# The first v of an attention-times-value kernel: two halves with two semaphores, cast by two engines

## The chip, the cores and the metric

The kernel runs on one core of one Trainium2 chip. The metric is the device time of one execution in microseconds (us). Three runs of the kernel before gave 1054.49 to 1054.95 us, median 1054.9.

## The reference

```
attn_weights: [8, 12, 1024, 1024] float32
v:            [8, 12, 1024, 64]   float32
out = einsum('bhqs,bhsd->bhqd', attn_weights, v)   # float32
```

For each of the 96 heads a 1024x1024 matrix is multiplied by a 1024x64 matrix. The attention weights are 403 MB, v and the output 25 MB each.

## The kernel before, in words

**Tiling.** Four heads make a group (`NV` = 24 groups). A group's attention weights are handled in two units (`NU` = 48), each with half of the queries of the four heads. A partition holds 32 queries of one head, so that 128 partitions hold four heads; a unit has `G` = 16 query slots of each partition. One load of a unit (`load_attn`, L314 to L320) reads 8 MB of float32 and writes 4 MB of bf16 into one of two buffers `abf`: the transfer itself converts. It is issued by GpSimd (POOL), whose transfers run on the software queue, q0. The last two units are loaded in two halves.

**A unit.** PE waits for its buffer, then transposes the 16 slots in 16 groups of 4 matmuls (`transpose_g`, L130), which use the four PSUM banks 0 to 3 in turn. From group 4 on, PE waits for the copy that empties the bank (`s_cp`). DVE copies the groups 0, 2, 4, 5, 7 of each eight, ACT the others (`copy_g`, L254). In the first unit of a group PE also spreads v (`spread_v`, L145): v arrives as `vr`, in bf16, with 32 rows of each head spread over partitions, and is brought into the layout `vbf` by PE, DVE and ACT (L230). Then the previous unit's result is transposed back (L157) and copied to `osb` (L237), and the unit's products are made (L172) and copied to `ot` (L266).

**What sets the order.** Each engine has its own instruction queue. POOL issues loads 0 and 1 at once, builds the constants `ident` and `spread` with affine selects, and then runs a loop over n (L363 to L372): it waits until PE has done those of unit n's transposes that DVE copies (`s_t[True]`), and issues load n + 2 into the buffer that these have freed. In some steps it also issues a load of v for two groups (`load_v`, L322) or a store of results.

**The first v.** The v of the first two groups (eight heads) takes another way. SP (SyncE) loads it as float32 on the hardware queue, q1, into two free slots of `osb` (`v32`, from slot `V_SLOT` = 4): first the 128 rows of group 0 (`two` = 0), then group 1 (`two` = 1) as 96, 22 and 10 rows (L382 to L385). A row is 2048 elements, 8 KB. All four transfers count on one semaphore, `s_v0`. DVE clears `ident`, `spread` and `ot`, waits for all four (L305), casts both groups into `vr` at once (L306) and adds 2 to `s_vr`; only after that does it enter its loop over the units. PE waits for `s_vr` of at least 1 before it spreads group 0 (L195), and of at least 2 before it spreads group 1, in unit 2. After its four transfers SP adds to `s_free` and `s_half`, which ACT's copies to `osb` and PE's groups from 8 on wait for.

Of the kernel before, what the change touches and what calls it, by code (L numbers as in the profile page):

```python
# [10 lines left out]
def kernel(  # L11
# [18 lines left out]
    nc = tc.nc  # L30
# [7 lines left out]
    P = 128  # L38
# [15 lines left out]

    NO = 8 + 2
    V_SLOT = 4

    HALVED = NU - 2

    def slot(q):  # L60
        return q % NO
# [6 lines left out]
    v_2 = v.rearrange("b h q d -> (b h) q d").rearrange(  # L68
        "(hq two four) (p r) d -> hq (four p) two (r d)", two=2, four=VH, p=VP
    )  # L70

    def on_dve(g):
        return g % 8 in (0, 2, 4, 5, 7)

    def count_of(g):

        return sum(on_dve(x) == on_dve(g) for x in range(g + 1))
# [4 lines left out]
    with tc.tile_critical(sync_engine=mybir.EngineType.Pool, no_gpsimd_drain=True):  # L82
        sem = tc.alloc_semaphore
# [5 lines left out]
        vr = sb("vr", [P, 2, VB, SB * D], bf16)  # L89
        vbf = sb("vbf", [P, SB, VH, D], bf16)  # L90
        ot = sb("ot", [P, GH, P], fp32)
        osb = sb("osb", [P, NO, 2 * G, D], fp32)

        v32 = osb[:, ds(V_SLOT, 2)].rearrange("p n r d -> p (n r d)")
        bank = [nc.alloc_psum_tensor(f"bank{i}", [P, 512], fp32).ap() for i in range(8)]
        pt = [b.rearrange("p (k j) -> p k j", k=KW) for b in bank[:4]]
        po = bank[4:6]
# [2 lines left out]

        s_abf = [sem(f"s_abf{i}") for i in range(2)]
        s_second = {n: sem(f"s_second{n}") for n in range(HALVED, NU)}
        s_v0, s_v = sem("s_v0"), sem("s_v")
        s_osb = [sem(f"s_osb{i}") for i in range(2)]
        s_held, s_end = sem("s_held"), sem("s_end")

# [11 lines left out]
        s_memset, s_const, s_vr = sem("s_memset"), sem("s_const"), sem("s_vr")  # L118
# [100 lines left out]
        transpose_back()  # L219


        def engine(dve):
            eng = nc.vector if dve else nc.scalar
            copy = nc.vector.tensor_copy if dve else nc.scalar.copy
            per = PER_DVE if dve else PER_ACT
            e = 0 if dve else 1

            def spread_copy(h, ps, count):
                eng.wait_ge(s_sp[e], count)
                copy(  # L230
                    out=vbf[:, :, h], in_=ps.rearrange("p (k d) -> p k d", k=SB)
                ).then_inc(s_vbf[e])

            def back_copy(rows, j0, jn, ps, count):

                eng.wait_ge(s_back, count)
                return copy(  # L237
                    out=rows.rearrange("p (half j) d -> p j half d", half=2)[:, ds(j0, jn)],
                    in_=ps[:, ds(0, jn * P)].rearrange("p (j half d) -> p j half d", half=2, d=D),
                )  # L240

            def rows_of(n):
                return osb[:, slot(n // 2), ds(n % 2 * G, G)]

            def back_copies(rows, count, free=None):
                if free is not None:
                    eng.wait_ge(s_free, free)
                for k in range(2):
                    last = back_copy(rows, 4 * k, 4, px[k], count + k + 1)
                last.then_inc(s_out)  # L250

            def copy_g(g, count):
                eng.wait_ge(s_t[dve], count)  # L253
                ins = copy(  # L254
                    out=at[:, g].rearrange("c k j two -> c (k j two)"),
                    in_=bank[g % 4].bitcast(bf16),
                )
                if g < G - 4:
                    ins.then_inc(s_cp[g])
                elif g == (G - 1 if dve else G - 2):  # L260
                    ins.then_inc(s_last[e])

            def product(count):

                eng.wait_ge(s_m[e], count)
                copy(  # L266
                    out=ot.rearrange("c j (h p) -> c h j p", h=VH)[:, ds(2 * e, 2)],
                    in_=po[e].rearrange("c (h j p) -> c h j p", h=2, j=GH),
                ).then_inc(s_ot[e])

            mine = [g for g in range(G) if on_dve(g) == dve]

            def unit(n, base, rows, free):

                of_t, of_sp, of_back, of_m = base
                for g in mine:
                    copy_g(g, of_t + (n * per + count_of(g)))
                if n % 2 == 0:
                    spread_copy(e, po[e], of_sp + (n + 1))
                    spread_copy(2 + e, px[e], of_sp + (n + 2))  # L280
                if not dve:
                    back_copies(rows, of_back + 2 * n, free)
                product(of_m + (n + 1))


            with nc.Fori(1, NV + 1, 1, engines=(DVE if dve else ACT,)) as it:  # L286
                base = [eng.snap(it * (2 * k) - 2 * k) for k in (per, 1, 2, 1)]
                rows = [None, None]
                if not dve:
                    for n, q in enumerate((it + (NO - 2), it + (NO - 1))):  # L290
                        rows[n] = osb[:, ds(eng.snap(q % NO), 1), ds((1 - n) * G, G)].rearrange(
                            "p one r d -> p (one r) d"
                        )
                    free = eng.snap((it + 1) // 2)
                unit(0, base, rows[0], None)
                unit(1, base, rows[1], None if dve else free)
            k = 1 - e
            back_copy(rows_of(NU - 1), 4 * k, 4, px[k], 2 * NU + k + 1).then_inc(s_fin[k])
# [3 lines left out]

        for h in range(2):
            nc.vector.memset(ot[:, :, ds(h * HP, HP)], 0.0).then_inc(s_ot[h])
        nc.vector.wait_ge(s_v0, 16 * 4)  # L305
        nc.vector.tensor_copy(out=vr.rearrange("p two b x -> p (two b x)"), in_=v32).then_inc(s_vr, 2)  # L306
        engine(True)
        engine(False)
        nc.scalar.wait_ge(s_held, 16 * (BY_SYNC - HELD_FROM) // 2)


        pool = nc.gpsimd

        def load_attn(n):  # L314
            pieces = [(0, G)] if n < HALVED else [(0, GH), (GH, GH)]
            for g0, gn in pieces:
                pool.dma_start(  # L317
                    out=abf[n % 2][:, ds(g0, gn)].rearrange("p g s -> p (g s)"),
                    in_=attn_q[n // 2][:, ds((n % 2 * G + g0) * S, gn * S)],
                ).then_inc(s_abf[n % 2] if g0 == 0 else s_second[n], 16)  # L320

        def load_v(iv):  # L322
            pool.dma_start(  # L323
                out=vr.rearrange("p two b x -> p two (b x)"), in_=v_2[iv]
            ).then_inc(s_v, 16)
# [10 lines left out]
        def store_2(q):  # L336
            store(q, 2, pool, s_osb[q // 2 % 2] if q < HELD_FROM else s_held)
# [5 lines left out]
            out=ident,  # L343
            in_=ident,
# [7 lines left out]
        for h in range(VH):  # L352
            pool.wait_ge(s_const, h + 1)
            pool.affine_select(  # L354
                out=spread[ds(h * VP, VP)],
                in_=spread[ds(h * VP, VP)],
# [6 lines left out]
        for n in range(NU - 2):  # L363
            q, i = n // 2, n % 2
            if i == 0 and q % 2 == 1 and q + 1 < NV:
                for s in s_sp:
                    pool.wait_ge(s, 2 * q + 2)
                load_v((q + 1) // 2)
            pool.wait_ge(s_t[True], (n + 1) * PER_DVE)
            load_attn(n + 2)  # L370
            if i == 0 and q % 2 == 0 and 0 < q <= HELD_FROM:
                store_2(q - 2)  # L372
        for q in range(HELD_FROM, BY_SYNC, 2):
# [4 lines left out]

        v32_2 = v32.rearrange("p (two x) -> p two x", two=2)
        for two, p0, pn in ((0, 0, P), (1, 0, 96), (1, 96, 22), (1, 118, 10)):  # L382
            nc.sync.dma_start(  # L383
                out=v32_2[ds(p0, pn), two], in_=v_2[0][ds(p0, pn), two]
            ).then_inc(s_v0, 16)  # L385
        nc.sync.sem_inc(s_free, NO // 2)
        nc.sync.sem_inc(s_half, HALVED)
        for k in range(1, NV // 2):
# [12 lines left out]
        for k in range(2):  # L401
# [3 lines left out]
            out=out_q[NV - 1], in_=osb[:, slot(NV - 1)].rearrange("p r d -> p (r d)")  # L405
# [32 lines left out]
```

## Time and profile before

| what | value |
|---|---|
| median of three runs | 1054.9 us (1054.49 to 1054.95) |
| the profiled execution | 1054.56 us |
| its span, first to last instruction | 1052.7 us |
| PE, matmuls busy | 737.3 us, 70% |
| PE, weight loads busy | 691.3 us, 66% |
| DVE busy | 388.5 us, 37% |
| ACT busy | 425.6 us, 40% |
| POOL busy | 45.0 us, 4% |
| HBM read and written | 427.82 MB and 25.17 MB |
| mean granted TensorE clock | 0.868 |

Issuing the 50 attn loads takes POOL 27.2 us. The median time from issue to landing of an attn load of 4096 KB is 33.5 us, of a later v load 17.2 us.

In a timeline line the columns are: start in us, duration in us, engine, line, operation, destination and source, shapes, count, and in brackets the idle time before it with what ended it. PE is the matmul row, PEld its weight loads, which overlap it. In the chain of waits the columns are start, duration, and what was waited for. "DMA" in the chain means the time from the issue of a transfer to its landing, which includes any time that the transfer stood in a queue. In the page's queue lines the numbers are packets, MB and the time that the packets took as a share of 16 DMA engines over the span (or over the window asked for).

### The profile page before, as it was taken

The numbers are of one execution on the slowest core, as the hardware profiler recorded it, in microseconds if no ns is written. First come the engines' busy times: TensorE is split into PE (matmuls) and PEld (weight loads), VectorE is DVE, ScalarE is ACT, GpSimd is POOL, SyncE is SP. The second block draws the span as 40 slices with busy tenths as digits, with TensorE's granted clock in tenths as the row PEclk, the third lists the DMA queues.
The fourth block names the chain that finished last, engine by engine and source line by source line (L and its number), as shares of the span: only waits on it lengthen the run. The fifth ranks groups of instructions, "written<-read, shape, count | busy, mean of one in ns | idle before, by whom it ended". The sixth has DMA issues, their size and how long they took to land.

```text
span 1052.7 us, 16498 instructions
## 1 busy us (share of the span) xinstructions
PE 737.3 (70%) x6920; PEld 691.3 (66%) x6920; DVE 388.5 (37%) x582; ACT 425.6 (40%) x505; POOL 45.0 (4%) x80
## 2 busy tenths in 40 slices
PE   0877677577686568766669657776776875875895
PEld 0776676576686567656668657765666865875884
DVE  0443343333353234333335324433333433532452
ACT  0454354343353334433335434433333443543452
POOL 1000000000000000000000000000000000000000
PEclk9989788898798888889879888888988988988898
DMA  9999999999999999999999999999999999999998
GB/s 237 221 219 214 217 252 217 219 217 247 228 213 254 215 219 257 218 218 225 240 220 217 258 217 219 257 214 217 246 224 219 218 208 229 215 210 222 214 215 344
DMA packets 13784, 240.17 MB, mean 228 GB/s; under 512 B 1237, under 2 KB 1237, under 8 KB 4053
## 3 DMA queue, kind: packets, MB, share of 16 engines
q0 software_dynamic: 12912, 233.84, 99.1%
q1 hardware_dynamic: 869, 6.29, 1.5%
q8 instruction: 2, 0.03, 0.0%
q14 instruction: 1, 0.01, 0.0%
HBM read 427.82 MB, written 25.17 MB: 430 GB/s over the span
## 4 chain that ended last, share of the span: by engine, by line
DMA 76%; PE 22%; issue 1%; DVE 0%; SPq 0%; ACT 0%; POOL 0%; DVEq 0%; POOLq 0%
DMA abf<-in_attn_weights_dram 73%; PE bank L130 21%; DMA osb<-in_v_dram 3%; PE bank L172 1%; PE bank L157 0%; DVE vbf L230 0%; SPq L383 0%; PE bank L145 0%; DVE at L254 0%; DVE osb L237 0%; ACT ot L266 0%; POOL abf L317 0%; DVEq L253 0%; DVE vr L306 0%; DVEq L286 0%
## 5 line engine op out<-in xcount | busy, mean ns | idle before, releaser
L130 PE MATMUL bank<-ident,abf 128*128 128x128 f32 x3072 | 453.5, 318 | 274.0 <-DMA abf<-in_attn_weights_dram 269.4
L130 PEld LDWEIGHTS bank<-ident,abf 128*128 128x128 f32 x3072 | 443.4, 214 | 287.4 <-DMA abf<-in_attn_weights_dram 281.2
L254 DVE COPY at<-bank 128x1024 bf16<-128x1024 bf16 x480 | 320.1, 689 | 466.1 <-PE bank L130 464.3
L254 ACT COPY at<-bank 128x1024 bf16<-128x1024 bf16 x288 | 288.7, 1012 | 404.3 <-PE bank L130 404.2
L172 PE MATMUL bank<-at,vbf 128*64 128x256 bf16 x3072 | 215.0, 278 | 0.0
L172 PEld LDWEIGHTS bank<-at,vbf 128*64 128x64 bf16 x3072 | 196.7, 108 | 13.3 <-DVE at L254 4.0
L266 ACT COPY ot<-bank 128x512 f32<-128x512 f32 x48 | 28.1, 586 | 174.0 <-PE bank L172 174.0
L266 DVE COPY ot<-bank 128x512 f32<-128x512 f32 x48 | 33.2, 692 | 151.3 <-PE bank L172 151.3
L157 PE MATMUL bank<-ident,ot 128*128 128x128 f32 x392 | 52.2, 276 | 32.9 <-DVE vbf L230 32.2
L157 PEld LDWEIGHTS bank<-ident,ot 128*128 128x128 f32 x392 | 43.4, 141 | 45.0 <-DVE vbf L230 44.0
L237 ACT COPY osb<-bank 128x512 f32 (+1 forms) x97 | 52.2, 589 | 27.3 <-PE bank L157 26.1
L317 POOL DMA_DIRECT2D abf<-in_attn_weights_dram x50 | 27.2, 545 | 690.9 <-PE bank L130 689.9
L230 DVE CAST vbf<-bank 128x512 bf16<-128x512 f32 x48 | 30.9, 686 | 6.6 <-PE bank L145 6.6
L254 ACT ACT_TABLE_LOAD x24 | 30.8, 1283 | 1.4 <-PEq L422 1.0
L230 ACT CAST vbf<-bank 128x512 bf16<-128x512 f32 x48 | 25.8, 589 | 11.8 <-PE bank L145 11.8
L145 PE MATMUL bank<-vr,spread 32*128 32x512 bf16 x384 | 25.7, 377 | 0.0
L323 POOL DMA_DIRECT2D vr<-in_v_dram x11 | 7.7, 704 | 238.4 <-PE bank L145 238.4
L145 PEld LDWEIGHTS bank<-vr,spread 32*128 32x128 bf16 x384 | 9.9, 92 | 6.9
L306 DVE CAST vr<-osb 128x4096 bf16<-128x4096 f32 x1 | 2.3, 2294 | 28.3 <-DMA osb<-in_v_dram 28.3
L330 POOL DMA_DIRECT2D out_dram<-osb x10 | 7.1, 715 | 29.8 <-ACT osb L237 29.8
L354 POOL TENSOR_SCALAR_AFFINE_SELECT spread<-spread 32x512 bf16<-32x512 bf16 x4 | 2.5, 628 | 0.6
L237 DVE COPY osb<-bank 128x512 f32<-128x512 f32 x1 | 0.7, 690 | 3.1 <-PE bank L157 3.1
(8 smaller groups left out, 2.1 us busy)
## 6 DMA issues: line engine op xcount, KB each, us to landing
abf<-in_attn_weights_dram POOLq DMA_DIRECT2D x46, 4096.0 KB, 33.5
out_dram<-osb POOLq DMA_DIRECT2D x10, 2048.0 KB, 29.5
vr<-in_v_dram POOLq DMA_DIRECT2D x11, 1024.0 KB, 17.2
abf<-in_attn_weights_dram POOLq DMA_DIRECT2D x4, 2048.0 KB, 24.0
out_dram<-osb SPq DMA_DIRECT2D x1, 2048.0 KB, 13.7
out_dram<-osb SPq DMA_DIRECT2D x2, 1024.0 KB, 11.4
osb<-in_v_dram SPq DMA_DIRECT2D x1, 1024.0 KB
osb<-in_v_dram SPq DMA_DIRECT2D x1, 768.0 KB
```

The source lines that it names most:

```text
L130: last = pe.matmul(out=pt[g % 4][:, k], lhsT=words[:, k], rhs=ident, is_transpose=True, start=(k == 0), stop=(k == KW - 1),)
L145: last = pe.matmul(out=ps, lhsT=spread[rows, b], rhs=vr[rows, two, b], start=(b == 0), stop=(b == VB - 1),)
L157: last = pe.matmul(out=ps[:, ds(j * P, P)], lhsT=ot[:, j0 + j], rhs=ident, is_transpose=True, start=(j == 0), stop=(j == jn - 1),)
L172: last = pe.matmul(out=outs, lhsT=vbf[:, 2 * kw + par, h], rhs=at[:, ds(half * GH, GH), kw, ds(h * VP, VP), par], start=(n == 0), stop=(n ...
L230: copy(out=vbf[:, :, h], in_=ps.rearrange("p (k d) -> p k d", k=SB)).then_inc(s_vbf[e])
L237: return copy(out=rows.rearrange("p (half j) d -> p j half d", half=2)[:, ds(j0, jn)], in_=ps[:, ds(0, jn * P)].rearrange("p (j half d) -> ...
L254: ins = copy(out=at[:, g].rearrange("c k j two -> c (k j two)"), in_=bank[g % 4].bitcast(bf16),)
L266: copy(out=ot.rearrange("c j (h p) -> c h j p", h=VH)[:, ds(2 * e, 2)], in_=po[e].rearrange("c (h j p) -> c h j p", h=2, j=GH),).then_inc( ...
L317: pool.dma_start(out=abf[n % 2][:, ds(g0, gn)].rearrange("p g s -> p (g s)"), in_=attn_q[n // 2][:, ds((n % 2 * G + g0) * S, gn * S)],).th ...
L323: pool.dma_start(out=vr.rearrange("p two b x -> p two (b x)"), in_=v_2[iv]).then_inc(s_v, 16)
L330: eng.dma_start(out=out_2[q // 2] if fours == 2 else out_q[q], in_=at_slot if fours == 2 else at_slot[:, 0], **({"single_packet": True} if ...
L354: pool.affine_select(out=spread[ds(h * VP, VP)], in_=spread[ds(h * VP, VP)], compare_op=mybir.AluOpType.not_equal, fill=1.0, base=0, patte ...
```

## The change

The transfers of the first v get two semaphores, one for each group of four heads. The first group's 128 rows are loaded as 48 and 80 rows, the second's as 96, 22 and 10 rows as before. DVE waits only for the first group's two transfers and casts only that group. The second group is cast by GpSimd: in the first step of its loop, after it has issued the third attn load (n = 0, load 2), it waits for the second group's three transfers and casts. Each cast adds 1 to `s_vr`.

```diff
+    FIRST_V = ((0, 48), (48, 80)), ((0, 96), (96, 22), (118, 10))
...
-        v32 = osb[:, ds(V_SLOT, 2)].rearrange("p n r d -> p (n r d)")
+        v32 = osb[:, ds(V_SLOT, 2)].rearrange("p n r d -> p n (r d)")
...
-        s_v0, s_v = sem("s_v0"), sem("s_v")
+        s_v0, s_v = [sem(f"s_v0_{i}") for i in range(2)], sem("s_v")
...
+        def cast_v(eng, two):
+            eng.tensor_copy(
+                out=vr[:, two].rearrange("p b x -> p (b x)"), in_=v32[:, two]
+            ).then_inc(s_vr)
...
-        nc.vector.wait_ge(s_v0, 16 * 4)
-        nc.vector.tensor_copy(out=vr.rearrange("p two b x -> p (two b x)"), in_=v32).then_inc(s_vr, 2)
+        nc.vector.wait_ge(s_v0[0], 16 * len(FIRST_V[0]))
+        cast_v(nc.vector, 0)
         engine(True)
...
             pool.wait_ge(s_t[True], (n + 1) * PER_DVE)
             load_attn(n + 2)
+            if n == 0:
+                pool.wait_ge(s_v0[1], 16 * len(FIRST_V[1]))
+                cast_v(pool, 1)
             if i == 0 and q % 2 == 0 and 0 < q <= HELD_FROM:
                 store_2(q - 2)
...
-        v32_2 = v32.rearrange("p (two x) -> p two x", two=2)
-        for two, p0, pn in ((0, 0, P), (1, 0, 96), (1, 96, 22), (1, 118, 10)):
-            nc.sync.dma_start(
-                out=v32_2[ds(p0, pn), two], in_=v_2[0][ds(p0, pn), two]
-            ).then_inc(s_v0, 16)
+        for two in range(2):
+            for p0, pn in FIRST_V[two]:
+                rows = ds(p0, pn)
+                nc.sync.dma_start(
+                    out=v32[rows, two], in_=v_2[0][rows, two]
+                ).then_inc(s_v0[two], 16)
```

## The prediction

> **What bounds the kernel now.** I read first the page's slices and queues, to see which resource is never free, then the chain of waits, then the first 68 us of the timeline and the transfers' landing times. From the page:
>
> ```profile
> span 1052.7 us, 16498 instructions
> ...
> DMA  9999999999999999999999999999999999999998
> ...
> q0 software_dynamic: 12912, 233.84, 99.1%
> q1 hardware_dynamic: 869, 6.29, 1.5%
> ...
> DMA abf<-in_attn_weights_dram 73%; PE bank L130 21%; DMA osb<-in_v_dram 3%; PE bank L172 1%; PE bank L157 0%; DVE vbf L230 0%; SPq L383 0%; PE bank L145 0%; DVE at L254 0%; DVE osb L237 0%; ACT ot L266 0%; POOL abf L317 0%; DVEq L253 0%; DVE vr L306 0%; DVEq L286 0%
> ```
>
> The DMA engines are busy in every slice; PE is busy 70% of the span. The last line seems to say otherwise: it gives PE's transposes (L130) 21%. The chain of waits shows where these shares come from, and the place that the change is about:
>
> ```profile
> 2.26 28.47 DMA osb<-in_v_dram
> ...
> 30.82 0.07 DVE vr L306
> ...
> 33.03 0.69 DVE at L254
> 33.73 0.04 issue
> 33.77 7.84 PE bank L130 x48
> ...
> 57.71 29.10 DMA abf<-in_attn_weights_dram
> 86.81 0.04 issue
> 86.85 7.96 PE bank L130 x64
> ```
>
> The chain walks from a landing to the issue of that transfer, and from there to the transposes that freed its buffer. It does not see that the transfer stood in a queue behind another one. So I check it with the landings, which are the starts of the transposes that a transfer released:
>
> ```profile
> 67.53 9.75 PEld L130 LDWEIGHTS bank<-ident,abf 128*128 128x128 f32 x64 [5.11 <-DMA abf<-in_attn_weights_dram]
> 86.85 7.76 PEld L130 LDWEIGHTS bank<-ident,abf 128*128 128x128 f32 x64 [1.81 <-DMA abf<-in_attn_weights_dram]
> 111.07 10.11 PEld L130 LDWEIGHTS bank<-ident,abf 128*128 128x128 f32 x64 [11.26 <-DMA abf<-in_attn_weights_dram]
> 130.40 7.83 PEld L130 LDWEIGHTS bank<-ident,abf 128*128 128x128 f32 x64 [1.46 <-DMA abf<-in_attn_weights_dram]
> ```
>
> The gaps are 19.32, 24.22 and 19.33 us; the long one has a later v load in it (4.9 us). They do not follow the issues, which come at irregular distances (57.71, 79.87, 95.10 us). A load lands 19.3 us after the load in front of it, whenever it was issued: that is a queue that never runs dry. The number that decides this case is therefore whether it runs dry near the third attn load. For the four loads of the first 60 us the trace gives
>
> ```profile
> DMA to landing us min/median/max: 25.6/28.4/46.0
> ```
>
> The longest is the second load: issued at about 2.1 us, it lands at 48.1. The third is issued at 41.91, **6.2 us before that landing**, and lands 25.6 us later, at 67.5, 19.4 after the second: the same spacing as later. The queue did not run dry there, to 0.1 us.
>
> **What DVE's wait costs now.** From the timeline:
>
> ```profile
> 29.24 3.69 PE L130 MATMUL bank<-ident,abf 128*128 128x128 f32 x16 [29.24 <-DMA abf<-in_attn_weights_dram]
> 30.82 2.29 DVE L306 CAST vr<-osb 128x4096 bf16<-128x4096 f32 x1 [28.25 <-DMA osb<-in_v_dram]
> 33.77 7.84 PE L130 MATMUL bank<-ident,abf 128*128 128x128 f32 x48 [0.84 <-DVE at L254]
> 41.91 0.57 POOL L317 DMA_DIRECT2D abf<-in_attn_weights_dram  x1 [35.66 <-PE bank L130]
> ```
>
> DVE waits for all of v until 30.8, casts until 33.1, and only then empties bank 0, which PE needs for group 4: PE stands 0.84 us. It also keeps PE's transposes slow for longer: they take 12.4 us (29.24 to 41.61), while unit 2, which starts after a pause too but has no such stall, needs 9.75 and 0.1.
>
> **The change, part by part.**
>
> *Removed: DVE's wait for the whole v, and half its cast.* The first 128-row half is 8 rows per DMA engine and goes first. The transfers of the first 6 us, the rate in 40 slices and the two queues:
>
> ```profile
> GB/s 0 0 0 0 0 0 0 0 0 0 0 0 164 55 0 109 109 273 164 218 328 437 218 655 164 655 164 546 328 546 328 546 328 546 328 546 328 382 382 437
> ...
> q1 hardware_dynamic: 178, 1.33, 60.9%
> q0 software_dynamic: 2, 0.07, 5.1%
> ```
>
> The first half is 128 rows of 8 KB and 16 completions, 144 packets; 178 had gone by 6.0 us. Adding up the slices of 0.15 us gives 1.05 MB at about 5.2 us. I take a landing of 6 us; the far bound is some 11 us, two attn packets later on a late engine. DVE's cast halves to about 1.2 us (2294 ns for 4096 elements) and is over by 8, bound 12. DVE is idle from 2.6 to 29, so it lies under that. Then DVE copies group 0 when PE has it, at 29.24 + 3.69/4 = 30.2, not 33.0, and bank 0 is free by 30.9, before PE asks at 32.9. PE gains between 0.84 us (the stall alone) and 2.5 (unit 2's 9.9 us, so transposes until 39.1). I take 2.5, since unit 2 is the nearest row. The third load is issued at 39.4 instead of 41.91. **Worth at the end: 0**, because the work in front of it in the queue lasts until 48.1 either way; the slack grows from 6.2 to 8.7 us. The fourth load's issue also comes earlier (unit 1 starts at its landing, 48.1, not at 49.4: 56.5 instead of 57.7) and stands behind the third until 67.5: 0.
>
> *Added on POOL: a wait and a cast of 128x2048, behind the third load's issue.* The wait is for v's second half, which lands at 30.7 now; one more packet in that queue may add one round behind an attn packet, 2.8 us, so 33.5 at most, before the 39.4 at which POOL gets there. The page has no GpSimd cast. Nearest rows: 512 elements of affine select take 628 ns, so 2.5 us; the dearest per element (128 in 0.29 us) gives 4.6; from below, DVE's 1.2. I take 2.5, because the shape is nearer. POOL is done at 42.5 (41 to 45). Behind the cast stands the fourth load, which waits for unit 1's transposes until 56.5: cover 11.5 us at the dear bound. The cast's result is first read in unit 2, after its transposes, at about 77.4: cover 32 us. DVE's half alone satisfies unit 0's wait. So 0.
>
> [...]
>
> *Changed: SP issues five transfers instead of four.* One issue is 0.41 us and 0.05 between: SP comes 0.46 us later to its two semaphore additions, needed by PE at group 8 and by ACT after 40 us: 0. One more completion packet on 16 engines costs between nothing and a row's 0.36 us (9.5% of 16 x 60 us over 256 rows); I take +0.05, as it carries almost no bytes. The bytes of each engine stay the same. The start may gain: in the line of rates above, the mean from 2.25 to 3.15 us is 200 GB/s, then 414, so 0.9 x (1 - 200/414) = 0.47 us of the DMA engines' time is lost while the engines join in. If this ramp goes with the first transfer's rows, 48 of 128 save 0.47 x 80/128 = 0.3; bounds 0 and 0.47. I take 0.3.
>
> [...]
>
> **Sum**, against the profiled execution (1054.56 us, span 1052.7): -0.3 + 0.05 and zeros = 1054.3. That execution is 0.34 below the median of the runs shown, so the forecast of the median is **1054.6**, its own range 1054.4 to 1055.3 (all bounds together).
>
> **Rivals.** About 0.2%, 2.1 us, is what a measurement of this kernel can tell from no change.
>
> *The chain is right, the earlier issue counts in full.* If the queue was emptier at 42 to 48 us than the landings say, for instance because the DMA engine that ends last had nothing left there, PE's 2.5 us reach the end: 1054.9 - 2.5 - 0.25 = **1052.1**. For it: the chain names v's transfer, the cast and PE's stall in a row. Against it: 19.4 us spacing there, 19.3 elsewhere.
>
> *Slower: GpSimd's cast holds back the third load's packets.* At the start POOL issues load 0 at 1.51 us, runs affine selects until 6.24, and the software queue had only 2 packets by 6.0 us: 4.5 us from issue to packets, perhaps because POOL's other work comes between. If packets of the third load are prepared behind the cast, they begin at 40.0 + cast + up to 4.5. With 2.5 that is 47.0, with 4.6 it is 49.1, 1.0 past the 48.1 where the queue runs dry. From a cast of 3.6 us on it costs, from 5.7 us it costs over 2.1; at 7 us, 51.5, 3.4 lost: **1058.1**. Against it: the start's delay may be the packets' preparation itself. [...]
>
> *It does not do what it says:* the first half lands as late as load 0, since both share the engines. Then DVE starts as now and all stays: 1054.9. The 178 packets speak against it. It is inside the forecast's answer.
>
> **How the numbers follow.** No change 0.64 (forecast 0.58, not doing what it says 0.06), earlier issue counts 0.22, cast holds the load 0.14. The range 1051.9 to 1056.5 holds all of the first, some 0.14 of the second and 0.02 of the third. Faster 0.22, same 0.64, slower 0.14.
>
> **What would show it.** DVE's cast near 6 to 8 us, half as long; no PE stall at 33; third load issued at 39 to 41; GpSimd's cast behind it, 2 to 5 us; and still transposes of unit 2 at 67 to 68 us and all later landings on the old grid. I am wrong if unit 2 starts more than 2 us before or after 67.5, or if the grid's spacing changes.

## The result, and the profile after

The changed kernel takes **1056.0 us** (median of 22 runs, 1055.4 to 1057.0) beside 1054.6 us for the kernel before (22 runs, 1053.76 to 1054.95): a ratio of 1.0014, interval 1.0007 to 1.0020. It is slower by some 1.4 us. That is less than the 0.2% named above, but with this many runs the interval leaves no change out. The profiled execution took 1055.76 us, 1.20 above that of the kernel before; 0.8 of that lies in the span from the first to the last instruction (1053.5 against 1052.7) and 0.4 outside it.

First the part that the change aimed at. From the timeline of the changed kernel:

```profile
7.57 1.23 DVE L224 CAST vr<-osb 128x2048 bf16<-128x2048 f32 x1 [5.00 <-DMA osb<-in_v_dram]
29.47 9.99 PE L131 MATMUL bank<-ident,abf 128*128 128x128 f32 x64 [29.47 <-DMA abf<-in_attn_weights_dram]
39.76 0.57 POOL L323 DMA_DIRECT2D abf<-in_attn_weights_dram  x1 [33.53 <-PE bank L131]
40.38 1.89 POOL L224 CAST vr<-osb 128x2048 bf16<-128x2048 f32 x1
```

All of it works. DVE casts the first group long before PE needs it, the stall of 0.84 us is gone (64 transposes in one piece), the third load is issued at 39.76 and not at 41.91, and GpSimd's cast stands behind it with no wait for v. In the chain of waits v's transfer, the cast and the spread are gone:

```profile
DMA abf<-in_attn_weights_dram 77%; PE bank L131 20%; PE bank L173 0%; PE bank L158 0%; POOL abf L323 0%; DVE osb L243 0%; ACT ot L272 0%; POOLq L443 0%; SPq L406 0%; POOLq L432 0%; POOLq L83 0%
```

And still the end is later. The landings say since when (starts of the transposes that a load released):

```profile
49.43 7.83 PEld L131 LDWEIGHTS bank<-ident,abf 128*128 128x128 f32 x64 [2.40 <-DMA abf<-in_attn_weights_dram]
68.61 9.10 PEld L131 LDWEIGHTS bank<-ident,abf 128*128 128x128 f32 x64 [6.14 <-DMA abf<-in_attn_weights_dram]
87.95 9.29 PEld L131 LDWEIGHTS bank<-ident,abf 128*128 128x128 f32 x64 [2.46 <-DMA abf<-in_attn_weights_dram]
112.19 9.45 PEld L131 LDWEIGHTS bank<-ident,abf 128*128 128x128 f32 x64 [9.74 <-DMA abf<-in_attn_weights_dram]
```

The spacing is the old one (19.18, 19.34, 24.24), but the grid stands 1.08 us later at unit 2 (68.61 against 67.53) and 1.10 at unit 3. The second load already lands at 49.4, where it landed at 48.1, and GpSimd's cast, from 40.4 to 42.3, has no load waiting on it. So the time is lost before the second load has landed, and the first 6 us of the transfers show where:

```profile
GB/s 0 0 0 0 0 0 0 0 0 0 0 0 218 382 273 0 218 328 437 382 382 109 55 164 164 55 382 0 109 218 218 382 218 218 382 109 328 164 273 164
...
q1 hardware_dynamic: 132, 0.95, 70.9%
```

Each number is the rate in 0.15 us, with every packet counted where it starts. Up to 3.15 us it is ahead of the kernel before: 0.39 MB have started, as much as the 48 rows. From 3.15 us on the mean is 195 GB/s where it was 414. By 6.0 us 0.95 MB of v had moved, not 1.33. The missing 0.38 MB at 414 GB/s are 0.92 us, near the 1.08 us of the grid. The first load lands only 0.23 us later (29.46 against 29.23): v's rows that are left over move between the packets of both loads (0.95 MB of v had moved by 6.0 us, 2.02 of the 2.10 MB by 30), and the delay stands in full only where both are through. At the last load it is 0.86 us (1032.55 against 1031.69).

### The profile page after: what moved, and what is told of

It is laid out like the page before. It is cut to its first block, busy times and chain, and to the rows that moved or that the text cites. A ratio compares the mean times of both kernels' runs of the same rounds, so it can differ in the third digit from the quotient of the medians.

```text
span 1053.5 us, 16499 instructions
## 1 busy us (share of the span) xinstructions
PE 733.0 (70%) x6920; PEld 687.3 (65%) x6920; DVE 387.6 (37%) x582; ACT 425.6 (40%) x505; POOL 47.0 (4%) x81
## 4 chain that ended last, share of the span: by engine, by line
DMA 77%; PE 21%; issue 1%; POOL 0%; DVE 0%; ACT 0%; POOLq 0%; SPq 0%
DMA abf<-in_attn_weights_dram 77%; PE bank L131 20%; PE bank L173 0%; PE bank L158 0%; POOL abf L323 0%; DVE osb L243 0%; ACT ot L272 0%; POOLq L443 0%; SPq L406 0%; POOLq L432 0%; POOLq L83 0%
```

## The experiments

Three theories stood against each other. *Rows:* a transfer of a part of the rows, all neighbours, moves at a lower rate than one of all 128 while nothing else is queued (195 GB/s against 414 above), and this makes the loss. *Completions:* each further transfer costs its engines some 1.4 us for its completion, which is the whole loss (1056.0 - 1054.6). These two expect the time of the kernel before when the first group goes in one transfer. *Casts:* the two casts, or the earlier third load, delay the queue.

**One transfer again (e1_whole, and once more as e6_again_whole).**

```diff
-    FIRST_V = ((0, 48), (48, 80)), ((0, 96), (96, 22), (118, 10))
+    FIRST_V = ((0, P),), ((0, 96), (96, 22), (118, 10))
```

> The changed kernel with the first group's 128 rows as one transfer again; two semaphores and the two casts stay. [...] Rival 'casts' (the two casts, GpSimd's above all, or the earlier third load delay the queue): stays at 1056.0, unit 2 at 68.6.

> The changed kernel with the first group's 128 rows as one transfer, once more: it stood 0.6 us above the kernel before at the median, with an interval that holds no change. 'Rows' alone: within 0.4 of the kernel before. If the two casts have a price of their own, 0.4 to 1.0 above it.

Measured: 1055.13 us (before 1054.51; ratio 1.0004, 0.9995 to 1.0013) and, in a second set of runs, 1054.95 (before 1054.62; 1.0004, 0.9995 to 1.0013). DVE's cast starts at 6.06 and 6.27 us, unit 2 at 67.22 and 67.61. Both intervals hold no change, so *casts* falls for the greater part of the loss, and the earlier third load (issued at 38.96 in the second of these) brings nothing. But the medians stand 0.6 and 0.3 us above the kernel before, the first outside the 0.4 that *rows* alone leaves room for, and the single runs show where this rest lies. The median span is 1052.8 and 1052.7 us here, beside 1052.6 and 1052.7 for the kernel before: inside the span nothing is lost, to 0.2 us. Outside the span, the time minus the span, the mean is 2.30 and 2.27 us, beside 1.96 and 1.93. All versions with two semaphores and two casts show this, the changed kernel too (2.25 to 2.33 us), and e2_split_only below, which has neither, does not (1.91). So about 0.35 us of the 1.4 come with the two semaphores and casts and not with the rows. Which of them costs it was not tried and stays open.

**The changed kernel beside it (e7_changed).**

> The changed kernel itself on the same chip as its neighbours here: 1.0 to 1.6 above the kernel before, and 0.8 to 1.4 above the one with 128 rows in one transfer. Theory 'casts' (now of the rest only): the distance to the 128-row kernel is under 0.5.

Measured: 1056.17 us, ratio to before 1.0014 (1.0005 to 1.0023), and 1.2 us above e6_again_whole on the same chip (1056.17 - 1054.95). The whole of this is in the span (median 1053.9 against 1052.7).

**The split alone (e2_split_only)**, in the kernel before:

```diff
-        for two, p0, pn in ((0, 0, P), (1, 0, 96), (1, 96, 22), (1, 118, 10)):
+        for two, p0, pn in ((0, 0, 48), (0, 48, 80), (1, 0, 96), (1, 96, 22), (1, 118, 10)):
...
-        nc.vector.wait_ge(s_v0, 16 * 4)
+        nc.vector.wait_ge(s_v0, 16 * 5)
```

> The kernel before with only its first transfer split into 48 and 80 rows; one semaphore, DVE casts all of v as before. 'Rows' and 'completions': 1056.0, unit 2 starts near 68.6. 'Casts': 1054.6, unit 2 at 67.5.

Measured: **1059.09 us**, ratio 1.0041 (1.0028 to 1.0055). Every theory missed that by 3 us and more. The timeline, DVE and POOL, then PE's weight loads:

```profile
37.73 2.29 DVE L306 CAST vr<-osb 128x4096 bf16<-128x4096 f32 x1 [35.16 <-DMA osb<-in_v_dram]
```

```profile
48.86 0.57 POOL L317 DMA_DIRECT2D abf<-in_attn_weights_dram  x1 [42.61 <-PE bank L130]
```

```profile
40.68 7.69 PEld L130 LDWEIGHTS bank<-ident,abf 128*128 128x128 f32 x48 [7.60 <-DVE at L254]
...
71.94 9.29 PEld L130 LDWEIGHTS bank<-ident,abf 128*128 128x128 f32 x64 [2.58 <-DMA abf<-in_attn_weights_dram]
```

All of v lands at 37.7 us, 6.9 us later than before, although only 0.4 MB more were left over at 6.0 us (0.90 MB had moved, not 1.33). By an estimate each row that did not get away before the attn packets came waits behind one of them, some 2.7 us a row (a load's 19.3 us are 8 packets on each engine, 2.4 us each, and the row's own 0.3 us at 437 GB/s for 16 engines). DVE casts late, PE stands 7.6 us, and the third load is issued at 48.86. The second lands at about 49.6 (the mean of the first two, 37.9 us from issue to landing, and the first at 29.79), so there were 0.7 us in hand, and the third lands 22.3 us behind it, not 19.3. The queue did run dry here. The rates from 44 to 56 us, in slices of 0.3 us:

```profile
GB/s 328 437 0 0 546 0 0 437 328 437 0 0 0 0 0 0 0 0 0 0 874 437 328 109 0 0 0 0 0 0 328 1311 109 0 0 0 0 0 328 1256
```

No packet starts between 47.0 and 50.0 us, and these 3.0 us are what the spacing has grown by; the second load itself lands 1.5 us later than before. Unit 2 is 4.4 us late, and so is the end (1059.09 - 1054.51 = 4.6). This shows two things. The slack that the prediction read was a real one, with an edge; and the two semaphores and casts of the change are what keeps the late second group off the path. They cover a lateness that the split makes.

**As many transfers, but over all rows (e3_columns).**

```diff
-    FIRST_V = ((0, 48), (48, 80)), ((0, 96), (96, 22), (118, 10))
+    FIRST_V = ((0, P, 0, 1024), (0, P, 1024, 1024)), ((0, 96, 0, 2048), (96, 22, 0, 2048), (118, 10, 0, 2048))
```

> The changed kernel with the first group's transfer split in two across the row (128 rows of the first 1024 elements, then 128 rows of the other 1024) in place of 48 and 80 rows: as many transfers and completions as in the changed kernel, but each reaches all partitions. 'Rows': 1054.6 +-0.4 (smaller packets may cost a little), DVE's cast near 5.5 to 6 us, unit 2 near 67.5. 'Completions': 1056.0, DVE's cast near 7.5, unit 2 near 68.6. 'Casts': 1056.0 with DVE's cast early.

Measured: 1055.02 us, ratio 1.0002 (0.9993 to 1.0011), DVE's cast at 6.43, unit 2 at 67.56. The same number of transfers and completions as in the changed kernel and some 1.0 us less (0.5 above its kernel before, the changed kernel 1.4): for *rows*, against *completions*.

**Four transfers of 32 rows (e4_four32).**

```diff
+    FIRST_V = ((0, 32), (32, 32), (64, 32), (96, 32)), ((0, 96), (96, 22), (118, 10))
```

> The changed kernel with the first group as four transfers of 32 rows: two more completions per engine than in the changed kernel. [...] 'Completions': three more than before at 1.4 us each, 1054.6 + 4.2 = 1058.8, DVE's cast past 10 us. 'Casts': 1056.0.

Measured: 1055.31 us, ratio 1.0006 (0.9997 to 1.0015), unit 2 at 68.26. *Completions* falls: 1058.8 was asked for. But *rows* missed too: it took four parts to be as late as two, with the changed kernel's 1056.0 us and a DVE cast near its 7.57 us, and the cast came at 21.75. The attn packets began earlier here (0.52 MB of them by 6.0 us, where the kernel before had 0.07; load 0 lands at 27.58, not at 29.2) and came in between the rows of the first group (0.52 MB of v by 6.0 us, not 1.33), so that fewer of them moved alone. Why they did is not settled; it makes this run a poor measure of the rate, and so v was measured by itself.

**v by itself (i1 to i4).** GpSimd issues the first attn load only when all of v is there:

```diff
+        for two in range(2):
+            pool.wait_ge(s_v0[two], 16 * len(FIRST_V[two]))
         load_attn(0)
         load_attn(1)
```

> Measures v's transfers by themselves: GpSimd issues the first attn load only when all of v has landed; first group as one transfer of 128 rows, second as 96, 22 and 10. DVE's cast starts when the first group has landed: 'rows' 6.0 us. [...]

> The same with the first group as 48 and 80 rows, no attn packets in the way. 'Rows': DVE's cast at 7.3 to 7.6 us as in the changed kernel, 1.3 to 1.5 later than with 128 rows; the first attn load is issued as much later. If attn packets were the cause of the late first group: 6.0 here.

> The same with 128 and 128 rows. 'Rows': first group at 6.0 us, second 2.5 later; first attn load issued at 8.6 to 9.0 us. If only the bytes counted, the same as with 96, 22 and 10 rows.

> The same with the first group as 32, 32, 32 and 32 rows. [...] 'Completions' would put it past 10 us.

The rates in slices of 0.3 us over the first 12 us, first of i3_both128 (128 and 128 rows), then i1_whole (128; 96, 22, 10), i2_split (48, 80; 96, 22, 10) and i4_four32:

```profile
GB/s 0 0 0 0 0 0 218 82 82 191 437 437 437 437 410 437 437 437 410 437 437 437 410 437 328 55 0 0 0 0 0 0 0 0 1529 218 0 0 0 0
```

```profile
GB/s 0 0 0 0 0 0 218 109 109 137 410 437 437 437 437 437 437 437 437 191 246 300 137 437 109 328 246 55 191 109 82 82 0 0 0 0 0 0 0 0
```

```profile
GB/s 0 0 0 0 0 0 328 109 246 437 218 82 219 137 82 355 137 300 246 218 273 191 301 164 355 273 191 328 164 355 109 328 246 137 218 164 82 0 0 0
```

```profile
GB/s 0 0 0 0 0 0 300 137 109 437 437 82 300 137 300 137 355 82 355 82 328 109 328 109 355 109 328 164 273 328 137 328 82 300 27 273 137 27 0 0
```

| | first group landed (DVE's cast) | all of v landed (first attn load issued) |
|---|---|---|
| i3_both128 | 5.80 | 8.87 |
| i1_whole | 6.26 | 11.86 |
| i2_split | 7.88 | 13.47 |
| i4_four32 | 7.93 | 13.28 |

The lines of i1_whole and then of i2_split:

```profile
6.26 1.23 DVE L224 CAST vr<-osb 128x2048 bf16<-128x2048 f32 x1 [3.69 <-DMA osb<-in_v_dram]
11.86 1.24 POOL L323 DMA_DIRECT2D abf<-in_attn_weights_dram  x2 [11.42 <-DMA osb<-in_v_dram]
```

```profile
7.88 1.23 DVE L224 CAST vr<-osb 128x2048 bf16<-128x2048 f32 x1 [5.31 <-DMA osb<-in_v_dram]
13.47 1.24 POOL L323 DMA_DIRECT2D abf<-in_attn_weights_dram  x2 [13.03 <-DMA osb<-in_v_dram]
```

This is the picture of the cause. A transfer of all 128 rows, once it has started up, runs at 437 GB/s, nearly flat (410 in four slices). In i1 the 96 rows begin near 5.0 us, when 1.05 MB have started, and from 5.7 us on the rate is little over half (a mean of 249 GB/s to 8.1 us). In i2 it is low from 3.0 us on (a mean of 205 GB/s to 6.6 us), and the first group lands 1.62 us later than in i1, all of v 1.61; the kernel ends 1.61 us later too (1062.58 against 1060.97, one run each). Attn packets have no part in it. i4 has two completions more on each engine than i2 (357 packets against 325) and lands with it (7.93 against 7.88, all of v 13.28 against 13.47), so completions have no price that shows. The expectations had the order of the first groups right; those of i1 and i2 came some 0.3 us past theirs (6.26 for 6.0, 7.88 for 7.6 at the latest), and i3's two landings were as expected or a little sooner.

The rate does not fall in proportion to the number of rows in a part. If it did, 32 rows would move at a quarter of it, four such transfers would be as late as four whole ones, 4 x 2.4 us (1.05 MB at 437 GB/s), and DVE's cast in i4 would come near 13 us (5.80 + 3 x 2.4), not at 7.93. Parts of 32 rows moved at 216 GB/s (i4 from 3.3 to 6.3 us), parts of 48 and 80 at 205 (i2), a whole group at 437. That the rate depends on which rows go together is shown. Why, no run shows: neighbouring rows of v are neighbours in HBM and in SBUF alike, and no run here parts the two sides.

**Both groups whole (e8_both128).**

```diff
+    FIRST_V = ((0, P),), ((0, P),)
```

> The changed kernel with both groups as one transfer of 128 rows each, two transfers in place of five. [...] Rival: the uneven 22 and 10 rows relieve the engines that end last, and without them the kernel is 0.5 to 1.5 slower.

Measured: 1054.86 us, ratio 1.0004 (0.9995 to 1.0013). By itself the second group is 3.0 us cheaper so (8.87 against 11.86), in the kernel nothing is seen of it (1054.86 against 1054.95 for e6_again_whole): most of its rows go between attn packets. That a transfer costs at its own rate only while nothing else is queued fits this, but was not measured by itself. The relief that the uneven rows might give is not seen either. No version tried is faster than the kernel before.

## Why the prediction was right or wrong

**What bounds the kernel: right.** The landings, not the chain, told the truth. The chain named v's transfer, the cast and PE's stall; the change takes all three off, and with the first group in one transfer, where nothing is lost in the span, nothing is gained either (e1_whole, e6_again_whole).

**The earlier third load is worth 0: right.** 39.76, 39.83 and 38.96 us instead of 41.91, with no gain. The rival "the chain is right" (1052.1) falls. PE's gain was a little less than taken, 39.5 for the end of its transposes against 39.1. One point was too simple: the queue does not run dry when the second load has landed but earlier. A load issued into an empty queue lands 22.4 us after its issue (i3_both128, 8.87 to 31.27), 3.1 more than the spacing, so by this estimate only about 3 of the 6.2 us in hand could be spent. In e2_split_only 0.7 were left, and the queue stood empty for 3.0.

**GpSimd's cast: right.** It took 1.89 us where 2.5 was taken, had no wait, and stopped nothing. The rival "the cast holds back the third load" (1058.1) falls: the third load lands 19.2 us after the second (68.61 - 49.43), the old spacing. Its time takes a cast of 7 us, which no run shows.

**Five transfers instead of four: here the prediction failed.** The step said that the bytes of each engine stay the same, that one more completion costs +0.05, and that a faster start saves 0.3. The bytes do stay the same (2.10 MB of v in the first 60 us, before and after) and the completion does cost next to nothing (i4 against i2). The faster start is there too: 0.39 MB by 3.15 us against 0.21. But the step priced the transfer as if the rate did not depend on which rows go together. It does: the first group alone moves at about 205 instead of 437 GB/s, and lands 1.62 us later by itself. In place of -0.25 us the term is about +1.2 (e7_changed against e6_again_whole). A second, smaller part stands nowhere in the sum: the 0.35 us outside the span that come with the two semaphores and casts, whose cause is open. The base moved as well: the forecast started from 1054.9, the median of three runs, and 22 runs give 1054.6. With these, 1054.6 + 1.2 + 0.35 is 1056.15, beside 1056.0 measured. The forecast's sign was wrong, and 1056.0 lies outside its own range (1054.4 to 1055.3). That the change is within 0.2% was forecast and came true, but partly by luck: nothing of this loss was in the working.

The bound of that step was missing on the side of a loss: it looked at the number of packets and at the ramp, and no row of the trace of before was read for a transfer with fewer rows. There was none that shows its rate plainly: the 96 rows begin shortly before the attn packets, and most of the second group goes between these.

**The first group as late as load 0: wrong**, as forecast; it landed at 7.6 us, a little past the 6 taken and within the bound of 11.

## What to carry to other kernels

A chain of waits that runs from a transfer's landing to its issue hides the queue in front of it: check the spacing of the landings, and take a wait off such a chain only if the transfer that it releases comes too late for the queue. Splitting a load by rows to get its first part sooner about halved its rate here while it was alone in the queues (205 GB/s in i2_split, 437 in i1_whole); if a split is needed, split along the row, so that each part still covers all 128 partitions (e3_columns: cast at 6.43 us, not 7.57). What shares its engines with a queue of large packets can get much later when a little more of it is left over: v landed 6.9 us later in e2_split_only for 0.4 MB, by the estimate above some 2.7 us for each row on an engine.

## What the runs showed of the hardware that was not expected

- 128 rows of 8 KB to all partitions move at 437 GB/s (i1_whole, i3_both128), parts of 32, 48 or 80 neighbouring rows one after another at about half of it (205 GB/s in i2_split, 216 in i4_four32), although the 16 DMA engines are busy meanwhile (74.5% of their time in the first 12 us of i2_split, 57.3% in i1_whole, for the same 2.10 MB).
- The DMA engines were shown busy for longer with the same bytes: in the changed kernel v's queue took 12.4% of the engines' time in the first 60 us, for the same 2.10 MB that took 9.5% before. That is 1.7 us per engine, of which 1.0 reached the end of the span (1053.7 in the median, against 1052.7).
- An attn load into an empty queue lands 22.4 us after its issue (i3_both128), one behind another 19.3 us after that one. In e2_split_only the packets of a load issued at 48.86 us into an empty queue start at 50.0.
- GpSimd cast 128x2048 float32 to bf16 in 1.89 us, DVE in 1.23 us (the changed kernel).
- With four transfers of 32 rows (e4_four32) the attn packets began earlier than in the kernel before: 0.52 MB of them had moved by 6.0 us against 0.07, and load 0 landed at 27.58 us against 29.23. What lets them in sooner stays open.
- All versions with two semaphores and two casts take some 0.35 us more outside the span than the kernel before (2.25 to 2.33 us against 1.93 to 1.96). What takes this time stays open.
